# A fused decoder block on one core: weight sums of the head in shared buffers, attention values prepared later, scan outputs in the update's PSUM bank

## The chip, the core and the metric

The kernel runs on one core of a Trainium2 chip. The metric is device time in microseconds (us) of one execution. Each engine works through an instruction queue of its own in order: TensorE (PE in the profile) multiplies, VectorE (DVE) and ScalarE (ACT) work on elements and can read PSUM, the banks that TensorE writes, GpSimd (POOL) works on SBUF, and SyncE (SP) issues DMAs. Engines wait for each other by semaphores.

## The reference

One layer of a hybrid block, batch 1, 1024 tokens, width 1024, all float32. Two branches read the same normalised input:

```python
h = rmsnorm(x, norm_mix);  parts = split(h @ w_in)
# branch 1: forgetting attention, 8 heads of 128, softmax over causal logits with a decay bias
p = softmax(where(causal, q @ k.T * scale + (c[:, None] - c[None, :]), -inf));  y1 = p @ v
# branch 2: gated delta rule, 8 heads, in chunks of 64
u = u_hat - w @ state
o = q_dec @ state + attn @ u
state = state * g_last + k_dec.T @ u
# then: gated merge of the two branches with w_branch, w_out, residual, gated ConvFFN, final rmsnorm
```

## The kernel before

Every large product is made of three TensorE passes over operands that are split into a high and a low part (`split`, L106 the high part on ACT by a cast, L107 the low part by a subtraction on DVE or POOL). TensorE's instructions stand in the order in which the code issues them (`manual_schedule` at its engine); the other engines' orders are chosen by the tile scheduler from its own costs, except where `keep_in_program_order` pins an instruction. Waits follow from the tiles that instructions share; a PSUM tile here is a bank of 128x512 floats.

The stages, in us of the profiled span:

- **head_in**, 0 to about 143. Eight tiles of x are normalised and transposed. Token weights come in four groups `g` (tiles `vwr`, split into `vwh` on ACT and `vwl` on DVE or POOL); for each group `rows(g, t)` multiplies eight token tiles, 24 matmuls each (L570 to L572), and stores the result. Three generators are taken between these rows: `scalars()` (decays; its last part transposes `rt` on TensorE, L700), `block_sums` (L362, sums of blocks for the next stage), and `prepare_merge`. The last loads all of `w_branch` (16 tiles of 512 KB into `raw`, four buffers, L998), makes four sums for each pair of tiles on DVE (`weight_sums`, L982 to L985) and stores them to DRAM (`ms`, L1004), for a stage 1000 us later. Loads and stores of it are pinned in SP's order.
- **project**, about 143 to 830: the input projections by a Strassen scheme (products L156), weights streamed through `wr` (L125, three buffers of pool `stream`), split on ACT (`oh`) and POOL (`ol`), sums of weight blocks `ws` on DVE (L202).
- **mix**, about 830 to 1101: attention and scan woven together. `fox` yields 26 steps a head (`probs`: logits L1102 to L1104 into a small PSUM tile `ms`, a maximum by DVE L1109, exponentials on ACT L1115, scaling on ACT L1118 or, for late tiles `p`, on POOL L1121; `attend`: transposes L1142, splits into `ph` and `pl`, products L1133 into `ya`). `fox_values` prepares the values of a head after their load: `vf` a copy, `vh` a cast on ACT, `vl` a subtraction on POOL.
- Beside it run two `stream`s of the scan, four heads each, 8 chunks `n` a head. A chunk takes three steps. Step 1: `us[0:P]` = kT·st on TensorE (L1256), then DVE makes `sr` (L1258). Step 2: `us[P:2P]` = xt·r (L1261), ACT copies it to `su` (L1263), and TensorE puts qd·st into another bank, `op` (L1266). Step 3: `us[2P:3P]` = kt·u (L1269), DVE makes the next state `ss` from it (L1272, or a copy L1275 for the first chunk), TensorE adds aq·u to `op` (L1277), DVE copies `op` to `so` (L1278) and ACT squares it (`sjk`, L1280). From step 26 of the loop on, `mix` takes one step of one stream after each attention step, the streams by turns (L1341).
- PSUM in mix: `us` two banks, `op` two, `ya` one, `ms` three.
- Then merge, mix_out and the ConvFFN, to the end. The change does not touch their code.

Of the kernel before, what the change touches and what calls it, by code (L numbers as in the profile page):

```python
# [17 lines left out]
P = 128  # L18
# [69 lines left out]
class Block:  # L88
# [309 lines left out]
    def run(self):  # L398
        tc = self.tc

        def pool(stack, name, **kw):
            return stack.enter_context(tc.tile_pool(name=name, bufs=1, reuse_waits="tile", **kw))

        with ExitStack() as ctx:
            self.cp = ctx.enter_context(tc.tile_pool(name="const", bufs=1))
            self.dr = ctx.enter_context(tc.tile_pool(name="scratch", bufs=1, space=DRAM))
            self.constants()
            ctx.enter_context(tc.manual_schedule(engines={mybir.EngineType.PE}))
            psum, left, right = ExitStack(), ExitStack(), ExitStack()

            def banks(small, mm=0, conv=0):
                psum.close()
                if mm:
                    self.mm = pool(psum, "ps_mm", space=PSUM)
                else:
                    self.acc = pool(psum, "ps_acc", space=PSUM)
                self.ms = pool(psum, "ps_ms", space=PSUM)
                self.nms, self.nmm, self.ms_tag, self.ncv = small, mm, "ms", conv


            banks(8)
            blk = self.blocks(pool(right, "hn", side="right"), ("11", "21", "22"))
            blk = self.head_in(blk, right)
            banks(2, 4, 2)
            self.st = pool(right, "stream", side="right")
            self.wt = pool(right, "weights", side="right")
            self.nw = 4
            self.sx = pool(right, "sums", side="right")
            self.cx = pool(right, "outputs", side="right")
            self.nc_ = 3  # L430
            self.project(blk, lambda: pool(left, "fox_in"))
            right.close()

            banks(3)
            self.st = pool(ctx, "stream2", side="right")
            so, sc = ExitStack(), ExitStack()
            self.so = pool(so, "so", side="right")
            zs, bs = ExitStack(), ExitStack()
            self.z = []

            def merge_pools():
                left.close()
                self.wt = pool(ctx, "weights2")
                for half, stack in ((1, left), (0, zs)):
                    zp = pool(stack, f"z{half}")
                    self.z.insert(0, [zp.tile([P, 512], F32, name=f"z{half}{e}") for e in range(KD)])
                self.merge_first(pool(bs, "br0"))

            self.mix([pool(left, f"fox{i}") for i in range(4)], pool(sc, "scan", side="right"), merge_pools)
            sc.close()  # L450

            psum.close()
            self.mm = self.ms = pool(psum, "ps_merge", space=PSUM)
            self.nms, self.ms_tag = 4, "b"
            self.br.append(pool(bs, "br1"))

            def merge_last():
                so.close()
                self.br.append(pool(bs, "br2"))
            self.merge(merge_last)  # L460
            bs.close()
            banks(2, 6)
            first = ExitStack()
            blk = self.blocks(pool(right, "hn2", side="right"), ("22",))
            blk.update(self.blocks(pool(first, "hn2a", side="right"), ("11", "21")))
            jobs, lead, ready = self.mix_out(blk, zs, lambda: pool(left, "hn2t"))

            self.sx = self.cx = pool(left, "sums2")
            self.nc_ = 3
            rest = []  # L470

            def down_inputs():
                first.close()
                return pool(right, "down_in", side="right")

            def down_main():
                left.close()
                return pool(left, "down")
            down = self.ffn_down(down_inputs, down_main, blk["22"])
            self.ffn_up(pool(left, "up"), jobs, blk, lead, ready, rest, down)  # L480
            for r in rest:
                finish(r)
            psum.close()
            self.mm = pool(psum, "ps_mm3", space=PSUM)
            finish(down)
            left.close()
            right.close()
            psum.close()
# [52 lines left out]
    def head_in(self, blk, right):  # L541
# [3 lines left out]
        with tc.tile_pool(name="hin", bufs=1) as pool, ExitStack() as px:  # L545
# [8 lines left out]
            def wgroup(g, eng):  # L554
                wh = pool.tile([P, KD * VGW], F32R, tag="vwh", bufs=2, name="vwh")
                wl = pool.tile([P, KD * VGW], F32R, tag="vwl", bufs=2, name="vwl")
                for q in range(4):
                    sl = slice(q * 2 * VGW, (q + 1) * 2 * VGW)
                    wr = pool.tile([P, 2 * VGW], F32, tag="vwr", bufs=3, name="vwr")
                    nc.sync.dma_start(wr, a["w_tok"][g][:, sl])  # L560
                    self.split(wh[:, sl], wl[:, sl], wr, eng)
                return wh, wl
# [57 lines left out]
            sums = self.prepare_merge(pool)  # L620
            for g in range(1, NVG):
                w = wgroup(g, nc.gpsimd)
                take(scalars, 1)
                for t in range(NT):
                    rows(g, t, *w)
                    take(sums, 1)
                    if t % 4 == 2 and g < 3:
                        sl = slice((2 * (g - 1) + t // 4) * P, (2 * (g - 1) + t // 4 + 1) * P)
                        self.block_sums(blk, whole("12", sl), whole("22", sl), sl, pool)
# [4 lines left out]
    def scalars(self):  # L634
# [16 lines left out]
        with tc.tile_pool(name="scal", bufs=1) as pool:  # L651
# [24 lines left out]
            nc.tensor.matmul(ps[:, 0:P], self.tri, gf, start=True, stop=True)  # L676
            ps2 = self.small()
            nc.tensor.matmul(ps2[:, 0:P], self.ones, gf, start=True, stop=True)
            cum, tot = tw("cum"), tw("tot")
            v.tensor_copy(cum.rearrange("p h t -> p (h t)"), ps[:, 0:P])  # L680
            v.tensor_copy(tot.rearrange("p h t -> p (h t)"), ps2[:, 0:P])
            carry = tl("carry")
            nc.gpsimd.memset(carry, 0.0)
            for t in range(1, NT):
                v.tensor_tensor(carry[:, :, t:t + 1], carry[:, :, t - 1:t], tot[:, H:, t - 1:t], ALU.add)
            rt = tw("rt")
            v.tensor_copy(rt[:, 0:H], cum[:, 0:H])
            v.scalar_tensor_tensor(rt[:, H:], cum[:, H:], -1.0, carry, op0=ALU.mult, op1=ALU.subtract)
            v.tensor_copy(self.gc, cum[:, 0:H])
# [297 lines left out]
    def prepare_merge(self, pool):  # L987
# [5 lines left out]
        for br in range(2):  # L993
            for k in range(4):
                raws = []
                for half in range(2):
                    t = pool.tile([P, 1024], F32, tag="raw", bufs=4, name="raw")
                    self.tc.keep_in_program_order(nc.sync.dma_start(t, a["w_branch"][KD * br + 4 * half + k]))  # L998
                    raws.append(t)
                yield  # L1000
                r0, r1 = raws
                self.weight_sums(r0[:, left], r1[:, left], r0[:, right], r1[:, right])
                for d, t in zip(self.ms_d[br][k], raws):
                    self.tc.keep_in_program_order(nc.sync.dma_start(d, t))  # L1004
                yield
# [49 lines left out]
    def fox_values(self):  # L1055
        raw = self.vl.bitcast(F32)
        self.nc.gpsimd.tensor_copy(self.vf, raw[:, 3::4, :])
        for sl in (slice(0, 4), slice(4, 8)):
            self.split(self.vh[:, sl], self.vl[:, sl], raw[:, sl], self.nc.gpsimd)

    def fox_bias(self, h):
        nc = self.nc
# [101 lines left out]
    def fox(self, pools, scan_pool):  # L1164
# [5 lines left out]
        for h in range(H):  # L1170
            pts = [] if h else self.pts
            for t in range(len(pts), NT):
                yield from self.probs(h, t, pts)
                if t == (3 if h else 4):
                    self.fox_values()
            for half in range(2):
                for i, _ in enumerate(self.attend(h, half, pts)):
# [15 lines left out]
    def mix(self, fp, pool, before_last):  # L1193
        tc, nc, a = self.tc, self.nc, self.a
        self.yf_d, self.yg_d = ([self.dr.tile([P, S], F32, name=f"{n}{h}") for h in range(H)] for n in ("yfd", "ygd"))
        if True:
# [50 lines left out]
            def scan(h):  # L1247
# [2 lines left out]
                sumo = self.so.tile([P, NB], F32, tag="sumo", bufs=3, name="sumo")  # L1250
                st = None
                for n in range(NB):
                    us = self.acc.tile([P, 512], F32, tag="us", bufs=2, name="us")
                    r = vb[:, n, :]
                    if n:
                        nc.tensor.matmul(us[:, 0:P], kT[:, n, :], st, start=True, stop=True)  # L1256
# [4 lines left out]
                    nc.tensor.matmul(us[:, P:2 * P], xt[:, n, :], r, start=True, stop=True)  # L1261
                    u = pool.tile([P, P], F32, tag="su", bufs=4, name="su")
                    nc.scalar.copy(u, us[:, P:2 * P])  # L1263
                    op = self.acc.tile([P, 512], F32, tag="op", bufs=2, name="op")
                    if n:
                        nc.tensor.matmul(op[:, 0:P], qd[:, n, :], st, start=True, stop=False)  # L1266
                    yield
                    if n < NB - 1:
                        nc.tensor.matmul(us[:, 2 * P:3 * P], kt[:, n, :], u, start=True, stop=True)  # L1269
                        s2 = pool.tile([P, P], F32, tag="ss", bufs=6, name="ss")  # L1270
# [3 lines left out]
                        else:  # L1274
                            nc.vector.tensor_copy(s2, us[:, 2 * P:3 * P])  # L1275
                        st = s2
                    nc.tensor.matmul(op[:, 0:P], aq[:, n, :], u, start=(n == 0), stop=True)  # L1277
                    nc.vector.tensor_copy(o[:, n, :], op[:, 0:P])  # L1278
                    jk = pool.tile([P, P], F32, tag="sjk", bufs=1, name="sjk")
                    nc.scalar.activation(jk, op[:, 0:P], AF.Square, accum_out=sumo[:, n:n + 1])  # L1280
                    yield
                outs[h] = o, sumo

# [52 lines left out]
            while take(fox, 1):  # L1336
# [1 line left out]
                    preps[i > 0] = prep(int(i > 0))  # L1338
                    take(preps[i > 0], 1)
                if i >= 26:  # L1340
                    take(streams[i % 2], 1)  # L1341
                elif i >= 8 and i % 2:
                    take(streams[0], 1)
                i += 1
# [585 lines left out]
```

## Time and profile before

| what | us |
|---|---|
| median of three runs | 2029.84 (2026.92, 2033.71, 2029.84) |
| profiled execution | 2033.09 |
| its span | 2031.3 |
| TensorE busy in it | 1924.7 |
| DVE, ACT, POOL busy | 1468.3, 1076.7, 976.6 |
| span 826 to 1101 (mix): TensorE busy | 247.4 of 275 |
| span 105 to 150 (end of head_in): TensorE busy | 31.9 of 45 |

The page of the profile gives one execution. "Busy" of TensorE includes matmuls that overlap, and a granted clock below 1.00 makes matmuls longer without making TensorE idle. A timeline row gives start, duration, engine, line, operation, tiles, and in brackets how long the engine had been idle and who released it. Views of waits list, for each line that an engine waited at, the instruction that it waited for, with the total, the number of times and the longest wait.

### The profile page before, as it was taken

The page shows a single profiled execution, that of the slowest core. Times are in us where ns is not written, and L with a number is a line of the kernel's source. Part 1 is how long each engine was busy: PE and PEld are TensorE (multiplying, and loading weights), DVE is VectorE, ACT ScalarE, POOL GpSimd, SP SyncE. Part 2 cuts the span into 40 slices and gives each one's busy share as a digit, 9 for nine tenths or more (in the row PEclk, how much of TensorE's full clock was granted, in tenths as well). Part 3 has the DMA queues.
Part 4 walks back from the last instruction along what each step waited for, and adds up shares of the span by engine and source line. Part 5 has one row for each costly group of instructions (what it writes and reads, how often), then busy time and mean ns, then how long its engine had stood idle before and what let it go on. Part 6 is the DMA issues. An engine that isn't in the chain of part 4 may idle for free. (4 is left out here: it accounts for less than half of the span.)

```text
span 2031.3 us, 29170 instructions
## 1 busy us (share of the span) xinstructions
PE 1924.7 (95%) x9628; PEld 1605.3 (79%) x9628; DVE 1468.3 (72%) x2514; ACT 1076.7 (53%) x2354; POOL 976.6 (48%) x818
## 2 busy tenths in 40 slices
PE   7869999999999999898999899999999999999998
PEld 7867888888788788787888787777788888877886
DVE  8937677766999865576777798577866777777535
ACT  5325777763334454565666544466655555553234
POOL 5715665655555555356675143135566666530012
PEclk9979999999999999899999999999999999999999
DMA  4672444544333394765654853665343343368654
GB/s 163 202 274 84 153 146 128 159 148 150 119 106 116 104 316 163 239 218 184 209 205 133 297 172 109 200 211 166 137 142 134 110 151 120 114 231 328 219 191 161
DMA packets 179048, 350.95 MB, mean 173 GB/s; under 512 B 50448, under 2 KB 63056, under 8 KB 178896
## 3 DMA queue, kind: packets, MB, share of 16 engines
q1 hardware_dynamic: 178752, 348.56, 51.0%
q8 instruction: 76, 1.25, 0.3%
q10 hardware_dynamic: 144, 0.52, 0.1%
q14 instruction: 76, 0.62, 0.1%
HBM read 232.79 MB, written 116.23 MB: 172 GB/s over the span
## 5 line engine op out<-in xcount | busy, mean ns | idle before, releaser
L107 POOL TENSOR_TENSOR ol<-ws,oh 128x512 fp32r<-128x512 f32 x212 | 285.7, 1351 | 239.6 <-ACT oh L106 231.9
L107 POOL TENSOR_TENSOR ol<-wr,oh 128x512 fp32r<-128x512 f32 x165 | 230.0, 1397 | 280.6 <-ACT oh L106 199.0
L106 ACT CAST oh<-ws 128x512 fp32r<-128x512 f32 x212 | 130.9, 618 | 176.7 <-PE mm L156 165.0
L202 DVE TENSOR_TENSOR ws<-wr 128x512 f32<-128x512 f32 x106 | 106.7, 1007 | 152.1 <-DMA wr<-in_w_up_dram 73.3
L106 ACT CAST oh<-wr 128x512 fp32r<-128x512 f32 x204 | 123.5, 616 | 127.5 <-PE mm L156 79.1
L377 DVE SCALAR_TENSOR_TENSOR cv<-c,fw,cv 128x512 f32<-128x512 f32 (+2 forms) x176 | 127.4, 748 | 16.0 <-ACT cv L372 14.6
L377 DVE SCALAR_TENSOR_TENSOR cv<-c,cw,cv 128x511 f32<-128x511 f32 (+2 forms) x144 | 106.0, 749 | 6.2 <-ACT cv L372 4.3
L156 PE MATMUL mm<-b11h,oh 128*128 128x512 f32 x216 | 85.6, 396 | 12.9 <-ACT oh L106 12.9
L961 DVE TENSOR_TENSOR invt<-invz 128x399 f32<-128x399 f32 (+50 forms) x114 | 94.8, 846 | 0.4
L258 ACT COPY x<-mm 128x512 f32<-128x512 f32 x158 | 92.0, 582 | 5.4 <-PE mm L156 4.5
L156 PE MATMUL mm<-b22h,oh 128*128 128x512 f32 x216 | 85.9, 398 | 8.2 <-ACT x L258 8.2
L156 PE MATMUL mm<-bt1h,oh 128*128 128x512 f32 x216 | 85.2, 395 | 5.8 <-ACT x L258 5.7
L107 DVE TENSOR_TENSOR ol<-wd,oh 128x512 fp32r<-128x512 f32 x66 | 46.4, 706 | 58.7 <-ACT oh L106 58.7
L156 PE MATMUL mm<-bt4h,oh 128*128 128x512 f32 x216 | 85.5, 396 | 2.7 <-DVE c L300 2.7
L156 PE MATMUL mm<-bt4l,oh 128*128 128x512 f32 x216 | 86.3, 399 | 0.0
L156 PE MATMUL mm<-b22l,oh 128*128 128x512 f32 x216 | 86.1, 398 | 0.0
L156 PE MATMUL mm<-b21l,oh 128*128 128x512 f32 x216 | 86.0, 398 | 0.0
L156 PE MATMUL mm<-b11l,oh 128*128 128x512 f32 x216 | 85.7, 397 | 0.0
L156 PE MATMUL mm<-b11h,ol 128*128 128x512 f32 x216 | 85.3, 395 | 0.1
L156 PE MATMUL mm<-bt2l,oh 128*128 128x512 f32 x216 | 85.1, 394 | 0.3 <-DVE bt2l L107 0.3
L156 PE MATMUL mm<-bt1l,oh 128*128 128x512 f32 x216 | 84.9, 393 | 0.0
L156 PE MATMUL mm<-bt4h,ol 128*128 128x512 f32 x216 | 84.8, 392 | 0.0
(402 smaller groups left out, 6391.6 us busy)
## 6 DMA issues: line engine op xcount, KB each, us to landing
wr<-in_w_up_dram SPq DMA_DIRECT2D x43, 512.0 KB, 3.7
wr<-in_w_gdn_dram SPq DMA_DIRECT2D x24, 512.0 KB, 3.9
wr<-in_w_out_dram SPq DMA_DIRECT2D x24, 512.0 KB, 4.3
s<-hy SPq DMA_DIRECT2D x44, 256.0 KB, 3.1
s<-z SPq DMA_DIRECT2D x44, 256.0 KB, 3.6
wd<-in_w_down_dram SPq DMA_DIRECT2D x44, 256.0 KB, 5.9
b22h<-s SPq DMA_DIRECT2D x44, 256.0 KB, 2.8
b22l<-s SPq DMA_DIRECT2D x44, 256.0 KB, 3.2
```

Of the source, the lines that this page charges most:

```text
L106: nc.scalar.copy(hi, src)
L107: (lo_eng or nc.vector).tensor_tensor(lo, src, hi.bitcast(F32), ALU.subtract)
L156: self.nc.tensor.matmul(ps, lhs[:, sl], rhs[:, k, :], start=(first and k == 0 and i == 0), stop=(k == 3 and i == 2), skip_group_check=True)
L202: v.tensor_tensor(t, x, y, op)
L258: nc.scalar.copy(t, x)
L377: nc.vector.scalar_tensor_tensor(t[:, lo:], c[:, 512 * j + lo - s:512 * (j + 1) - s], w[:, n - 1 - s:n - s], t[:, lo:], op0=ALU.mult, op1= ...
L961: nc.vector.tensor_tensor(tv, z[:, m:n, 0:n].to_broadcast([P, r, n]), z[:, m, c0:c1].unsqueeze(2).to_broadcast([P, r, n]), ALU.mult))
```

## The change

Four edits, with no change to what is computed.

1. **Head.** The pool `stream` is opened before `head_in`. In `prepare_merge` every other pair of tiles (odd `k`) uses its `wr` buffers, three of them, and `raw` has two buffers in place of four; `vwr` has two in place of three. The sums are taken from row (1, 4) on, four rows later. The last part of `scalars` (transpose of `rt`) comes after row (3, 4) in place of ahead of group 3; three of its tiles reuse older ones.
2. **Attention values.** `fox_values` is called after the logits of tile 6 in place of tile 3 (4 for head 0), and the two casts to `vh` are pinned in ACT's order.
3. **Scan outputs.** `op` is no longer a bank of its own but the last quarter of `us`. `us` has three banks, `ms` four. The matmul qd·st moves from step 2 to step 3, behind kt·u and the reading of it by DVE.
4. **Streams.** From step 26 on, both streams take a step after every second attention step, in place of one stream after each.

```diff
@@ mix's banks
-            banks(3)
+            banks(4)
@@ wgroup
-                    wr = pool.tile([P, 2 * VGW], F32, tag="vwr", bufs=3, name="vwr")
+                    wr = pool.tile([P, 2 * VGW], F32, tag="vwr", bufs=2, name="vwr")
@@ head_in
-                take(scalars, 1)
+                if g < 3:
+                    take(scalars, 1)
                 for t in range(NT):
                     rows(g, t, *w)
-                    take(sums, 1)
+                    if g > 1 or t > 3:
+                        take(sums, 1)
+                    if (g, t) == (3, 4):
+                        finish(scalars)
@@ prepare_merge
-                    t = pool.tile([P, 1024], F32, tag="raw", bufs=4, name="raw")
+                    if k % 2 == 0:
+                        t = pool.tile([P, 1024], F32, tag="raw", bufs=2, name="raw")
+                    else:
+                        t = self.st.tile([P, 1024], F32, tag="wr", bufs=3, name="raw")
@@ fox_values
-            self.split(self.vh[:, sl], self.vl[:, sl], raw[:, sl], self.nc.gpsimd)
+            self.tc.keep_in_program_order(self.nc.scalar.copy(self.vh[:, sl], raw[:, sl]))
+            self.nc.gpsimd.tensor_tensor(self.vl[:, sl], raw[:, sl], self.vh[:, sl].bitcast(F32), ALU.subtract)
@@ fox
-                if t == (3 if h else 4):
+                if t == 6:
                     self.fox_values()
@@ scan
-                    us = self.acc.tile([P, 512], F32, tag="us", bufs=2, name="us")
+                    us = self.acc.tile([P, 512], F32, tag="us", bufs=3, name="us")
...
-                    op = self.acc.tile([P, 512], F32, tag="op", bufs=2, name="op")
-                    if n:
-                        nc.tensor.matmul(op[:, 0:P], qd[:, n, :], st, start=True, stop=False)
                     yield
+                    old = st
                     if n < NB - 1:
                         nc.tensor.matmul(us[:, 2 * P:3 * P], kt[:, n, :], u, start=True, stop=True)
...
-                    nc.tensor.matmul(op[:, 0:P], aq[:, n, :], u, start=(n == 0), stop=True)
-                    nc.vector.tensor_copy(o[:, n, :], op[:, 0:P])
+                    op = us[:, 3 * P:]
+                    if n:
+                        nc.tensor.matmul(op, qd[:, n, :], old, start=True, stop=False)
+                    nc.tensor.matmul(op, aq[:, n, :], u, start=(n == 0), stop=True)
+                    nc.vector.tensor_copy(o[:, n, :], op)
@@ mix
                 if i >= 26:
-                    take(streams[i % 2], 1)
+                    if i % 2:
+                        for s in streams:
+                            take(s, 1)
```

In the changed file the scan's lines are L1264 (kT·st), L1266 (`sr`), L1269 (xt·r), L1271 (`su`), L1275 (kt·u), L1278 and L1281 (`ss`), L1285 (qd·st), L1286 (aq·u), L1287 (`so`), L1289 (`sjk`); the logits are L1110 to L1112, the casts to `vh` L1066.

TensorE's queue in the middle of mix, where each stream ends a chunk. Before, xt·r and qd·st of one stream (L1261, L1266), then logits and four transposes (L1302), then step 3 of the first stream, logits, step 3 of the second:

```order
L1261 MATMUL us<-sr,sxt 128x128 [waits DVE_49]
L1266 MATMUL op<-ss,sqd 128x128 [waits Activation_49]
L1302 MATMUL ms<-ident,so 128x128 [waits DVE_49,PE_49,Pool_49]
L1302 MATMUL ms<-ident,so 128x128 x3
L1102 MATMUL ms<-kh,qh 128x320 [waits DVE_49,PE_49]
L1103 MATMUL ms<-kl,qh 128x320
L1104 MATMUL ms<-kh,ql 128x320
L1269 MATMUL us<-su,skt 128x128 [waits Activation_49]
L1277 MATMUL op<-su,saq 128x128
L1102 MATMUL ms<-kh,qh 128x384 [waits DVE_49]
L1103 MATMUL ms<-kl,qh 128x384
L1104 MATMUL ms<-kh,ql 128x384
```

And now:

```order
L1110 MATMUL ms<-kh,qh 128x384 [waits DVE_49]
L1111 MATMUL ms<-kl,qh 128x384
L1112 MATMUL ms<-kh,ql 128x384
L1275 MATMUL us<-su,skt 128x128 [waits Activation_49]
L1285 MATMUL us<-ss,sqd 128x128 [waits DVE_49]
L1286 MATMUL us<-su,saq 128x128
L1275 MATMUL us<-su,skt 128x128 [waits Activation_49]
L1285 MATMUL us<-ss,sqd 128x128 [waits DVE_49]
L1286 MATMUL us<-su,saq 128x128
L1110 MATMUL ms<-kh,qh 128x384 [waits PE_49]
L1111 MATMUL ms<-kl,qh 128x384
L1112 MATMUL ms<-kh,ql 128x384
```

Both streams' step 3 stand together, qd·st has moved behind kt·u, and it now waits for DVE, where the aq·u that stood in its place waited for nothing. What it waits for is DVE's reading of the bank's third quarter (L1278), which the matmul just ahead of it has filled. This wait stands at 48 matmuls L1285 and, for the first chunk of each head, at 8 matmuls L1286 (behind L1281).

ACT's queue at the values of the fourth attention head. `vh` and `vl` are the values, `p` the probabilities of a tile, `su` the scan's copy. Before:

```order
L1118 ACTIVATE p_9621<-p_9621,mm 128x128 [waits DVE_49]
L106 CAST vh<-vl 128x512 [waits DMAHW5_49]
L106 CAST vh<-vl 128x512
L1115 ACTIVATE p_9650,mm<-p_9650,mm 128x256 [waits DVE_49,Pool_49]
L1263 COPY su<-us 128x128 [waits PE_49]
L1115 ACTIVATE p_9667,mm<-p_9667,mm 128x384 [waits DVE_49,Pool_49]
```

And now:

```order
L1123 ACTIVATE p_9697,mm<-p_9697,mm 128x768 [waits DVE_49]
L1271 COPY su<-us 128x128 [waits PE_49] x2
L106 CAST ph<-ms 128x512 [waits PE_49]
L1123 ACTIVATE p_9732,mm<-p_9732,mm 128x896 [waits DVE_49]
L1066 CAST vh<-vl 128x512 [waits DMAHW4_49]
L1066 CAST vh<-vl 128x512
L1123 ACTIVATE p_9788,mm<-p_9788,mm 128x1024 [waits DVE_49]
```

The two casts, and with them the wait for the values' load, moved from behind the first tile's probabilities to behind the seventh's.

SP's queue at the end of head_in: stores of the sums (`ms`), stores of the rows (`vd`), and the first three weight loads of the next stage (`wr`). Before:

```order
L1004 DMA ms_689<-raw 128x1024 [waits DMAHW2_49,DVE_49]
L580 DMA vd<-vev 128x262 [waits DMAHW3_49,Activation_49]
L1004 DMA ms_690<-raw 128x1024 [waits DMAHW4_49,DVE_49]
L1004 DMA ms_691<-raw 128x1024 [waits DMAHW6_49,DMAHW5_49,DVE_49]
L580 DMA vd<-vev 128x262 [waits Activation_49]
L580 DMA vd<-vev 128x262 [waits DMAHW7_49,Activation_49]
L580 DMA vd<-vev 128x262 [waits DMAHW0_49,Activation_49]
L125 DMA wr<-in_w_gdn_dram 128x1024 [waits DMAHW1_49,Pool_49]
L125 DMA wr<-in_w_gdn_dram 128x1024 [waits DMAHW2_49,PE_49]
L125 DMA wr<-in_w_gdn_dram 128x1024 [waits DMAHW3_49]
```

And now:

```order
L125 DMA wr<-in_w_gdn_dram 128x1024 [waits DMAHW5_49]
L580 DMA vd<-vev 128x262 [waits DMAHW4_49,Activation_49]
L1010 DMA ms_825<-raw 128x1024 [waits DVE_49]
L580 DMA vd<-vev 128x262 [waits DMAHW6_49,Activation_49]
L1010 DMA ms_826<-raw 128x1024 [waits DMAHW7_49,DVE_49]
L1010 DMA ms_827<-raw 128x1024 [waits DMAHW0_49,DVE_49]
L1010 DMA ms_828<-raw 128x1024 [waits DMAHW1_49,DVE_49]
L713 DMA gr<-rows 128x512 [waits DMAHW2_49,PE_49]
L713 DMA gr<-rows 128x512 [waits DMAHW3_49]
L125 DMA wr<-in_w_gdn_dram 128x1024 [waits DMAHW4_49,DMAHW0_49]
L125 DMA wr<-in_w_gdn_dram 128x1024 [waits DMAHW5_49,DMAHW1_49]
```

The first of the three loads moved ahead of the last four stores of the sums; the second and third stand behind them, and now wait for stores out of the buffers that they fill.

More of the change, by code (lines that the diff above doesn't have):

```diff
@@ L422, in run @@
             blk = self.blocks(pool(right, "hn", side="right"), ("11", "21", "22"))
+            self.st = pool(right, "stream", side="right")
             blk = self.head_in(blk, right)
             banks(2, 4, 2)
-            self.st = pool(right, "stream", side="right")
             self.wt = pool(right, "weights", side="right")
@@ L678, in scalars @@
             nc.tensor.matmul(ps2[:, 0:P], self.ones, gf, start=True, stop=True)
-            cum, tot = tw("cum"), tw("tot")
+            cum, tot, rt = z, az, e
             v.tensor_copy(cum.rearrange("p h t -> p (h t)"), ps[:, 0:P])
@@ L685, in scalars @@
                 v.tensor_tensor(carry[:, :, t:t + 1], carry[:, :, t - 1:t], tot[:, H:, t - 1:t], ALU.add)
-            rt = tw("rt")
             v.tensor_copy(rt[:, 0:H], cum[:, 0:H])
@@ L1276, in scan @@
                         st = s2
-                    nc.tensor.matmul(op[:, 0:P], aq[:, n, :], u, start=(n == 0), stop=True)
-                    nc.vector.tensor_copy(o[:, n, :], op[:, 0:P])
+                    op = us[:, 3 * P:]
[3 more added lines that the diff above has]
+                    nc.vector.tensor_copy(o[:, n, :], op)
                     jk = pool.tile([P, P], F32, tag="sjk", bufs=1, name="sjk")
-                    nc.scalar.activation(jk, op[:, 0:P], AF.Square, accum_out=sumo[:, n:n + 1])
+                    nc.scalar.activation(jk, op, AF.Square, accum_out=sumo[:, n:n + 1])
                     yield
```

## The prediction

> **What bounds the kernel now.** I read the page first: the busy line.
>
> ```profile
> PE 1924.7 (95%) x9628; PEld 1605.3 (79%) x9628; DVE 1468.3 (72%) x2514; ACT 1076.7 (53%) x2354; POOL 976.6 (48%) x818
> ```
>
> TensorE is busy for 1924.7 of 2031.3 us. The change removes no matmul, so it can act only on the 106.6 us in which TensorE is idle, on the few us at a lower clock, or by adding idle time. Idle time in TensorE's queue is end-to-end time, since nothing overtakes in it. The second view is the table of windows over the stages that are edited (columns: length; busy time of PE, PEld, DVE, ACT, POOL with counts; granted clock; DMA share; GB/s).
>
> ```profile
> 50.00:105.00 55.00, 47.04 (x385) 46.85 (x384) 54.58 (x64) 19.89 (x42) 43.05 (x26) 0.94 0.56 189
> 105.00:135.00 30.00, 25.20 (x192) 25.00 (x190) 11.18 (x17) 3.79 (x10) 0.00 (x0) 0.90 0.96 347
> 135.00:150.00 15.00, 6.72 (x22) 4.97 (x23) 4.04 (x4) 4.79 (x9) 5.55 (x4) 0.61 0.63 210
> 826.00:1101.00 275.00, 247.40 (x1751) 223.13 (x1750) 191.26 (x711) 180.13 (x507) 157.60 (x173) 0.96 0.60 197
> ```
>
> Mix has 27.6 us of idle TensorE in 275, the head some 21 between 50 and 150. The third view is the list of TensorE's waits, first for the end of the head, then for mix (total, times, longest).
>
> ```profile
> PE mm L156 <- ACT oh L106: 12.9, 1, 12.9
> PE ms L700 <- DVE rt L688: 8.0, 1, 8.0
> ```
>
> ```profile
> PE us L1269 <- ACT su L1263: 8.3, 5, 3.9
> PE ms L1142 <- POOL p L1121: 4.8, 4, 2.5
> PE ms L1142 <- DVE pl L107: 4.3, 7, 2.0
> PE ms L1102 <- DVE mx L1109: 1.8, 4, 0.8
> ...
> PE us L1256 <- DVE ss L1272: 0.3, 1, 0.3
> ```
>
> So mix's idle time is scattered over short waits, the longest group being kt·u, which waits for ACT's copy `su`. DVE's update `ss` is hardly waited for (0.3). The view of its line says how long DVE itself sat idle for it.
>
> ```profile
> L1272 DVE SCALAR_TENSOR_TENSOR ss<-ss,egl,us x48: 328/342/350, 856.6 to 1099.4; 128x128 f32<-128x128 f32 x48
> its engine sat idle before it (us, times) until:
>   PE us L1269: 10.8, 8
> ```
>
> **Scan outputs in the bank of the update.** This is the term that decides. Before, the order was kt·u, then at once aq·u into another bank; DVE turned kt·u into `ss` meanwhile, and `ss` was needed a step later. Now qd·st writes the bank that DVE is reading, and the order rows of the change show it waiting for DVE; it stands directly behind kt·u. So TensorE has nothing to do from the end of kt·u to the end of `ss`, 56 times (48 at L1285, 8 at L1286 for first chunks). The trace of before holds this round trip, only not as a wait. Three cases from the timeline, with kt·u (L1269), aq·u (L1277) and `ss`:
>
> ```profile
> 916.49 0.38 PE L1269 MATMUL us<-su,skt 128*128 128x128 f32 x2
> 916.71 0.39 PE L1277 MATMUL op<-su,saq 128*128 128x128 f32 x2
> 916.91 0.35 DVE L1272 SCALAR_TENSOR_TENSOR ss<-ss,egl,us 128x128 f32<-128x128 f32 x1 [0.23 <-PE us L1269]
> ...
> 945.37 0.58 PE L1269 MATMUL us<-su,skt 128*128 128x128 f32 x2
> 945.74 0.64 PE L1277 MATMUL op<-su,saq 128*128 128x128 f32 x2
> 946.13 0.33 DVE L1272 SCALAR_TENSOR_TENSOR ss<-ss,egl,us 128x128 f32<-128x128 f32 x1
> ...
> 1026.50 2.19 DVE L1049 SCALAR_TENSOR_TENSOR ql<-ql,qh 128x1024 fp32r<-128x1024 f32 x1 [1.47 <-ACT qh L1048]
> 1027.00 0.39 PE L1277 MATMUL op<-su,saq 128*128 128x128 f32 x2
> 1028.82 0.33 DVE L1272 SCALAR_TENSOR_TENSOR ss<-ss,egl,us 128x128 f32<-128x128 f32 x1
> ```
>
> The stall is the end of `ss` less the time at which the next matmul started. In the first case DVE was idle and waiting: 916.91 + 0.35 - 916.71 = 0.55 us. That is the floor. In the second DVE came 0.17 us later than that: 946.13 + 0.33 - 945.74 = 0.72. In the third an operation of 2.19 us stood ahead: 2.15. DVE was idle and waiting in only 8 of the 48 cases. Lower bound: 56 x 0.55 = 31 us. Upper: the same difference, row by row over all 56 pairs; the first and the last:
>
> ```profile
> 847.82 0.63 PE L1277 MATMUL op<-su,saq 128*128 128x128 f32 x2
> 848.06 0.29 DVE L1275 COPY ss<-us 128x128 f32<-128x128 f32 x1
> ...
> 1099.15 0.39 PE L1277 MATMUL op<-su,saq 128*128 128x128 f32 x2
> 1099.35 0.35 DVE L1272 SCALAR_TENSOR_TENSOR ss<-ss,egl,us 128x128 f32<-128x128 f32 x1 [1.36 <-PE us L1269]
> ```
>
> They give 0.53 and 0.55, and the 56 sum to 47.6, a mean of 0.85. I take 0.72, the second case and near the middle of 0.55 and 0.85, since DVE catches up on its queue while TensorE stands: **+40 us**.
>
> Could it cost nothing? Only if the wait were not there or were met beforehand. The trace shows that engines are kept apart by bank and not by need:
>
> ```profile
> ACT sjk L1280 <- DVE so L1278: 11.6, 10, 1.8
> ```
>
> ACT squares what DVE copies, both only read `op`, and still ACT waited 10 times for the copy. The Trainium skill ("PSUM — Partial Sum Buffer", section "PSUM bank collisions raise a hardware error") states the rule: two engines may not touch the same bank and partitions at once, not even in separate columns, so guard by bank. By that rule the sum contains the +40; by the address alone, under which the fourth quarter is free while the third is read, the term would be 0 and the total some 20 us below the time before. No run here shows a collision.
>
> What else belongs to this part: the third `us` bank and the fourth `ms` bank add slack. The wait of the transposes L1142 for `pl` (4.3) is a wait for a small bank to come free, so a fourth one takes most of it. The waits for `mx` (1.8) and for POOL's `p` (4.8) are waits for engines that run behind; TensorE, coming 40 us later over the stage, meets part of them done. Of these 10.9 us I take away **-9**, with 0 and -19 (mix's whole idle time less the 8.3 below) as ends.
>
> **Attention values later.** The list of ACT's waits in mix, then the timeline at the longest wait of kt·u:
>
> ```profile
> ACT vh L106 <- DMA vl<-vd: 12.4, 6, 4.4
> ```
>
> ```profile
> 942.45 1.14 ACT L106 CAST vh<-vl 128x512 fp32r<-128x512 f32 x2 [4.41 <-DMA vl<-vd]
> 944.29 0.49 PE L1269 MATMUL us<-su,skt 128*128 128x128 f32 x2 [3.93 <-ACT su L1263]
> ```
>
> ACT stands at the cast for the values' load, `su` is queued behind, TensorE behind that. With the cast three tiles of logits later (six of the 205 attention steps that fill the 275 us, so some 8 us), the load is there and the wait goes: nearly all of the 8.3 us, **-8**. What is late next is `vl`: its two subtractions on POOL (16 of them, 1280 ns each) now stand among the scalings of `p` for the last tiles, and the first product with `vl` follows soon after.
>
> ```profile
> L107 POOL TENSOR_TENSOR vl<-vl,vh 128x512 fp32r<-128x512 f32 x16 | 20.1, 1280 | 7.3 <-issue 4.9 <-ACT vh L106 2.4
> ```
>
> Two subtractions put the last scaling off by up to 2.6 us in each of seven heads, 18 us at worst; but POOL is idle for 117 of 275 us, and by then TensorE has 8 transposes and a few products to do that need neither. **+2**, with 0 and +6 as the ends I hold likely. Where the clock drops after the 3.93 us wait (below) another 1 us comes back: **-1**.
>
> **Streams together.** The number of steps is the same, and each stream still moves once in two attention steps. The pairing takes away the attention matmuls that stood between the two round trips, so the second one gets no cover from the first; this is in the 56. It is counted at nothing otherwise.
>
> **Head.** The waits of 8.0 and 12.9 are the targets. The rows:
>
> ```profile
> 101.64 1.83 POOL L107 TENSOR_TENSOR vwl<-vwr,vwh 128x524 fp32r<-128x524 f32 x1
> 104.39 0.45 PE L700 MATMUL ms<-ident,rt 128*128 128x128 f32 x1 [7.96 <-DVE rt L688]
> 132.65 1.05 SPq L1004 DMA_DIRECT2D ms<-raw  x2
> 138.10 1.35 SPq L125 DMA_DIRECT2D wr<-in_w_gdn_dram  x3
> 143.15 0.80 PE L156 MATMUL mm<-b11h,oh 128*128 128x512 f32 x1 [12.95 <-ACT oh L106]
> ```
>
> Without the transpose ahead of group 3, TensorE can start its rows when the last `vwl` is there. That was at 103.47, 0.9 us before it started anyway; with DVE relieved of the sums for four rows, this chain comes some 4 us earlier, and TensorE may finish its rows up to 8 us sooner. But the stage ends with the weights of project. Between 105 and 135 the DMA share is 0.96: 16.8 MB of `w_branch` in and out must pass (16 tiles of 512 KB each way), no less than before, and they start four rows later. One of the three first weight loads now passes ahead of the last stores, the other two stand behind them and must wait for stores out of their own buffers. Before, the first product came 5 us behind the issue of its load (143.15 - 138.10); with an issue near 130, ahead of the last stores, it would come at 135. The third, which needs a sum of two later weights, comes hardly earlier. I take **-3.5**, with +2 (loads later by the delay of the sums) and -9 as ends. Two buffers for `vwr` in place of three may cost 0.5 at the start.
>
> **Sum.** 40 - 9 - 8 + 2 - 1 - 3.5 + 0.5 = +21. On the profiled execution's 2033.09 that is 2054; on the median of 2029.84, 3.25 lower, it is **2051 us**, which is my forecast. A change under 0.3%, about 6 us (2023.7 to 2035.9), cannot be told from none here.
>
> **Rivals.** *The round trip is hidden, and the kernel gets faster.* Mechanism: at L1285 TensorE waits only for what is left of `ss`. If loading of weights and the pipeline's drain covered all but 0.2 us, the term is 11, and the sum 11 - 9 - 8 + 2 - 1 - 3.5 + 0.5 = -8, or with the head's better end -13.5: 2016 to 2022. It decides at (9 + 8 - 2 + 1 + 3.5 - 0.5) / 56 = 0.34 us for each round trip. Against it: the `ss` alone takes 0.34, and DVE's start after kt·u comes on top. 0.14.
>
> *The floor holds and the waits of before vanish.* 31 for the stalls, but mix's other waits go wholly (-19): 31 - 19 - 8 + 2 - 1 - 3.5 + 0.5 = 0 to +2, no change that can be told: 2030 to 2032. 0.09.
>
> *The clock falls as well.* After the wait of 3.93 the clock went down, after another of 1.35 it did not:
>
> ```profile
> 944.00:947.00 3.00, 2.71 (x14) 2.71 (x15) 2.54 (x14) 3.00 (x13) 3.00 (x4) 0.74 1.03 411
> 1010.00:1013.00 3.00, 3.00 (x21) 2.93 (x22) 3.00 (x15) 3.00 (x10) 1.11 (x1) 1.00 0.96 339
> ```
>
> A stall of 0.7 is too short for that alone, but two round trips stand side by side, with 0.6 us of matmuls between, and the upper ends are near 2 us. If a fall of some 3 us at half clock came ten times, at 1.5 us each, it would add 15: 2066. 0.12. The Trainium skill ("TensorE: Matmul & The Clock Gate") gives about 3.4 us as the idle window after which the clock is halved; by it the paired stalls cost no clock, which is why this is a rival and not the forecast.
>
> *The head's edit does nothing or harm* (+2 for -3.5): 2056, inside the forecast's range.
>
> **How the numbers follow.** Forecast 0.60 (own range 2038 to 2062: 0.55 to 0.85 us a round trip is -9 to +8, the rest the head and the absorbed waits), clock 0.12, no change 0.09, faster 0.14; 0.05 for a cost that I do not see, mostly on the slow side. Slower 0.77, same 0.09, faster 0.14. The range of 8 in 10 reaches from 2024, which leaves out most of the faster rival, to 2068.
>
> **What would show it.** In the changed profile the list of TensorE's waits in mix should have the lines L1285 <- DVE `ss` and L1286 <- DVE at its top, together 30 to 45 us, and mix should be 20 to 30 us longer with more idle TensorE; the wait of L1275 for `su` should be under 2 us, and `vh` <- DMA small. The first product of project should start near 135, with new waits for `ws` or `ol` before 150. I am wrong if those two lines sum to under 19 us (faster then), if mix's clock is under 0.93 (rival three), or if `vl` or the last `p` on POOL heads the list.

## The result and the profile after

The changed kernel is slower: 2065.44 us (2064.65 to 2067.66) against 2031.1 of the kernel before (four runs now), a ratio of 1.0173 with a 95% interval of 1.0153 to 1.0193. The forecast was slower, 2051, with a range of 2024 to 2068. One execution in this document, of the kernel with the head's edit alone, took 2935.40 at a granted clock of 0.61; its ratio leaves it out.

The profiled execution took 2066.07 with a span of 2064.4, 33.1 longer than before. Landmarks on TensorE place it: attention's last product came at 1099.8 before and at 1132.0 now, the first scan product of mix at 844.0 before and 840.6 now. So mix took 291.4 us in place of 255.8, **35.6 more**, what lies ahead of it 3.4 less, and what follows 0.9 more.

TensorE's waits in mix of the changed kernel (total, times, longest), to be held against the list of before:

```profile
PE us L1285 <- DVE ss L1278: 31.7, 46, 1.4
PE us L1275 <- ACT su L1271: 4.0, 2, 2.1
PE us L1286 <- DVE ss L1281: 3.4, 7, 1.0
...
PE ya L1141 <- POOL vl L1067: 1.8, 2, 1.2
...
PE us L1285 <- DVE mm L1122: 1.1, 2, 0.5
PE ya L1141 <- DVE pl L107: 0.8, 3, 0.5
...
PE us L1285 <- ACT su L1271: 0.7, 1, 0.7
PE ms L1110 <- DVE mx L1117: 0.7, 1, 0.7
PE us L1286 <- DVE mm L1122: 0.7, 1, 0.7
```

The two lines of the prediction head the list: at qd·st (L1285) and the first chunks' aq·u (L1286) TensorE waited 31.7 + 3.4 + 1.1 + 0.7 + 0.7 = 37.6 us. Of these, 36.9 stand at the 56 matmuls behind kt·u; the 0.7 put down to ACT stand at the last chunk of a head, where there is no kt·u. The waits of the transposes for `p` (4.8) are gone and those for `pl` fell from 4.3 to 0.8; kt·u's wait for `su` is halved, 8.3 to 4.0. Two such waits are left. At both, ACT has just made a late cast to `vh` (at 842.33 and 1077.85, 1.12 us for its two parts, with no wait for the load), ahead of the copy to `su`:

```profile
843.67 0.79 PE L1275 MATMUL us<-su,skt 128*128 128x128 f32 x2 [2.09 <-ACT su L1271]
...
1079.93 0.49 PE L1275 MATMUL us<-su,skt 128*128 128x128 f32 x2 [1.92 <-ACT su L1271]
```

But 36.9 less what vanished does not make 35.6. The windows over the same stretch of the program, before and after (length; busy time of PE, PEld, DVE, ACT, POOL; clock), show the rest:

```profile
843.50:1100.00 256.50, 233.35 (x1665) 212.44 (x1666) 179.49 (x666) 169.05 (x486) 151.50 (x167) 0.95 0.59 191
```

```profile
840.00:1132.30 292.30, 242.98 (x1666) 214.25 (x1666) 185.88 (x666) 172.86 (x489) 155.60 (x170) 0.96 0.52 169
```

TensorE's idle time rose from 23.2 to 49.3, 26.1 more, and its *busy* time rose by 9.6 with the same matmuls and no lower clock. Rows of one step tell why; kt·u, `ss`, qd·st:

```profile
904.60 0.39 PE L1275 MATMUL us<-su,skt 128*128 128x128 f32 x2
905.35 0.34 DVE L1278 SCALAR_TENSOR_TENSOR ss<-ss,egl,us 128x128 f32<-128x128 f32 x1
905.74 0.49 PE L1285 MATMUL us<-ss,sqd 128*128 128x128 f32 x2 [0.76 <-DVE ss L1278]
```

The pair at 904.60 ends at 904.99, but in an unbroken row the next pair would have started 0.22 after it, at 904.82 (as at 916.49 and 916.71 before). It started at 905.74: 0.92 late, of which the profile calls 0.76 idle. The other 0.16 is the pair's tail, which a following matmul would have overlapped. Over all 56 steps the lateness, row by row, sums to 46.7 us, 0.83 a step. So 46.7 came in, and to make 35.6 some 11.1 must have gone. The lists agree: outside the 56, TensorE idled for 23.2 before and for 49.3 - 36.9 = 12.4 now, 10.8 less.

### The profile page after: what moved, and what is told of

It is laid out like the page before. It is cut to its first block, busy times and chain, and to the rows that moved or that the text cites. A ratio compares the mean times of both kernels' runs of the same rounds, so it can differ in the third digit from the quotient of the medians.

```text
span 2064.4 us, 29115 instructions
## 1 busy us (share of the span) xinstructions
PE 1935.3 (94%) x9628; PEld 1607.5 (78%) x9628; DVE 1460.2 (71%) x2514; ACT 1078.8 (52%) x2354; POOL 973.5 (47%) x818
## 5 line engine op out<-in xcount | busy, mean ns | idle before, releaser
L202 DVE TENSOR_TENSOR ws<-wr 128x512 f32<-128x512 f32 x106 | 100.8, 951 | 149.6 <-DMA wr<-in_w_up_dram 78.0
L156 PE MATMUL mm<-bt2h,oh 128*128 128x512 f32 x216 | 84.5, 391 | 1.7 <-ACT oh L106 1.7
L156 PE MATMUL mm<-bt2h,ol 128*128 128x512 f32 x216 | 84.2, 390 | 1.0 <-POOL ol L107 1.0
```

What stands on the lines that cost most here:

```text
L156: self.nc.tensor.matmul(ps, lhs[:, sl], rhs[:, k, :], start=(first and k == 0 and i == 0), stop=(k == 3 and i == 2), skip_group_check=True)
L202: v.tensor_tensor(t, x, y, op)
```

## Experiments

"Ratio" is to the kernel before on the same chip, with its 95% interval.

### The wait taken out, in two ways, and put in alone

The first kernel gives `op` its own bank again and leaves the other three edits:

```diff
-            banks(4)
+            banks(3)
-                    us = self.acc.tile([P, 512], F32, tag="us", bufs=3, name="us")
+                    us = self.acc.tile([P, 512], F32, tag="us", bufs=2, name="us")
...
+                    op = self.acc.tile([P, 512], F32, tag="op", bufs=2, name="op")
+                    if n:
+                        nc.tensor.matmul(op[:, 0:P], qd[:, n, :], st, start=True, stop=False)
                     yield
...
```

> The changed kernel with the scan outputs back in a bank of their own (two banks us, two op, three ms, and the product of the query with the state back in step 2); the head, the later values and the streams together stay. Theory (the wait of 56 matmuls for DVE's reading of the same bank is the whole loss, 47 us with the overlap that each of them breaks): the lines L1285/L1286 <- DVE vanish, the time falls by 47 less up to 12 for older waits that the stalls had absorbed: 2018 to 2030. Rival one (streams stepping together cost the time, as no attention stands between their products): stays over 2045. Rival two (later values put POOL's work in the way): stays over 2045, with waits for vl or p at the top.

Measured: 2040.98, ratio 1.0030 (1.0013 to 1.0047). The wait's lines vanished and 1.4% came back, but the kernel stayed slower than before, well above the range. Both rivals' "over 2045" failed too, but the sign that rival two named, `vl` at the top, is there:

```profile
PE ya L1141 <- POOL vl L1067: 11.3, 6, 4.2
PE us L1277 <- ACT su L1271: 4.1, 4, 1.9
PE ms L1150 <- DVE pl L107: 3.4, 4, 1.9
```

The products with `vl` now wait for POOL's subtractions, 11.3 us where the changed kernel had 1.8.

The second kernel keeps the shared bank and moves only the order of issue within step 3:

```diff
+                    op = us[:, 3 * P:]
                     if n < NB - 1:
                         nc.tensor.matmul(us[:, 2 * P:3 * P], kt[:, n, :], u, start=True, stop=True)
+                    if n:
+                        nc.tensor.matmul(op, qd[:, n, :], old, start=True, stop=False)
+                    nc.tensor.matmul(op, aq[:, n, :], u, start=(n == 0), stop=True)
+                    if n < NB - 1:
                         s2 = pool.tile([P, P], F32, tag="ss", bufs=6, name="ss")
...
-                    op = us[:, 3 * P:]
-                    if n:
-                        nc.tensor.matmul(op, qd[:, n, :], old, start=True, stop=False)
-                    nc.tensor.matmul(op, aq[:, n, :], u, start=(n == 0), stop=True)
```

> The changed kernel with one thing moved: in step 3 TensorE's three products (update, query with state, attention with u) are issued ahead of DVE's reading, so that all banks are as in the changed kernel but no matmul waits for DVE within the step. Theory: the 56 waits vanish, DVE's ss comes 0.4 us later and nobody waits for it: 2014 to 2026, below the kernel before. Rival one: over 2045, since the streams still step together. A third way: ss is late then and the next step's product kT with the state waits for it, which would give back up to 20 us: 2030 to 2045.

Measured: 2034.08, ratio 1.0014 (0.9999 to 1.0028), above the theory's range. The time lies in that of the third way, but not by its mechanism: the DVE waits within the step are gone, and `ss`, read later, is waited for once, for 0.2 us. Again the sum of the "gains" that should remain is missing, and again `vl` heads the list:

```profile
PE ya L1141 <- POOL vl L1067: 7.4, 3, 4.3
PE us L1276 <- ACT su L1271: 6.2, 4, 1.9
PE ms L1150 <- POOL p L1129: 4.4, 3, 2.6
PE us L1264 <- ACT sjk L1290: 3.9, 2, 2.9
```

The last line is a cost of the shared bank itself: `op` now holds a bank of `us` until ACT has squared it, and kT·st of a later chunk waited for that bank 3.9 us where the kernel before shows no such wait.

The third kernel is the one before with the sharing alone (the diff's parts in `scan` and `banks`).

> The kernel before with the scan-output edit alone (op in the last quarter of us, three banks us, four ms, the query's product behind the update's); head, values and turns as before. Theory: 2031 + 47 less some 8 for waits that are absorbed, 2062 to 2078, with 56 waits for DVE of 35 to 40 us in the list. Rival one (it is the stepping together): 2031 to 2045. Rival two (values): 2031 to 2045.

Measured: 2083.09, ratio 1.0244 (1.0219 to 1.0269), above the theory's range.

```profile
PE us L1277 <- DVE ss L1270: 30.0, 45, 1.4
PE ya L1133 <- DVE pl L107: 4.9, 5, 1.7
PE us L1267 <- ACT su L1263: 4.5, 4, 2.3
PE us L1278 <- DVE ss L1273: 4.4, 7, 1.2
```

Mix took 303.9 us (843.4 to 1147.3), 48.1 more than before. That this is near the prediction's upper end for the stalls alone (47.6) does not mean that nothing was absorbed: its waits at these two lines are 37.2, its other idle time 17.8 where it was 23.2 before, and TensorE's busy time rose by 16.2, more than in the changed kernel, at a clock of 0.94. So one edit alone costs more than all four together.

### The other three edits, each alone on the kernel before, and the streams by turns

By turns means the changed kernel with its last edit undone:

```diff
-                    if i % 2:
-                        for s in streams:
-                            take(s, 1)
+                    take(streams[i % 2], 1)
```

> The changed kernel with the streams by turns again, all else kept. Theory: the round trip is the same for each step wherever it stands, 2058 to 2070, with 35 to 40 us of waits at L1285 and L1286. Rival one (the stepping together is the loss): 2018 to 2040.

Measured: 2072.55, ratio 1.0189 (1.0164 to 1.0213), 2.5 us above the theory's range. Pairing the streams is not the loss. The converse, the paired step alone on the kernel before:

> The kernel before with the streams stepping together alone. Theory: it counts for nothing by itself, 0.998 to 1.002. Rival (two scan steps side by side leave too little work between the links of a chain, so that sr, su and ss are waited for): 1.003 or more, with waits at kT with the state or at xt.

Measured: 2029.89, ratio 0.9995 (0.9981 to 1.0008): nothing.

The head's edit alone (the first of the four):

> The kernel before with the head's edit alone. Theory now (from the traces: the first product of project 6 us earlier, the third no earlier, as its weights are issued 3 us later): 0.999 to 1.002. Rival (the prediction's term, -3.5): 0.996 to 0.999.

Measured: 2029.6, ratio 0.9996 (0.9983 to 1.0009). It can't be told from nothing; the prediction's -3.5 (0.9983) lies at the edge of the interval. The traces of before and of the changed kernel show how the gain at the first product is lost. Before, SP's loads and TensorE:

```profile
138.10 1.35 SPq L125 DMA_DIRECT2D wr<-in_w_gdn_dram  x3
...
143.15 0.80 PE L156 MATMUL mm<-b11h,oh 128*128 128x512 f32 x1 [12.95 <-ACT oh L106]
...
157.09 0.50 PE L156 MATMUL mm<-bt1h,oh 128*128 128x512 f32 x1 [0.83 <-ACT x L258]
```

After:

```profile
131.47 0.33 SPq L125 DMA_DIRECT2D wr<-in_w_gdn_dram  x1
...
141.06 10.32 SPq L125 DMA_DIRECT2D wr<-in_w_gdn_dram  x3
...
136.99 0.80 PE L156 MATMUL mm<-b11h,oh 128*128 128x512 f32 x1 [13.73 <-ACT oh L106]
140.97 0.79 PE L156 MATMUL mm<-b11h,ol 128*128 128x512 f32 x1 [2.76 <-POOL ol L107]
150.49 0.50 PE L156 MATMUL mm<-bt2h,oh 128*128 128x512 f32 x1 [1.69 <-ACT oh L106]
152.18 0.50 PE L156 MATMUL mm<-bt2h,ol 128*128 128x512 f32 x1 [0.96 <-POOL ol L107]
157.32 0.39 PE L156 MATMUL mm<-bt1h,oh 128*128 128x512 f32 x1
```

The first product came 6.2 us earlier, since its load passed the stores. The next loads were issued at 141.06, 3 us later than before; three waits of 2.8, 1.7 and 1.0 follow, and by 157 the same product runs 0.2 later than before. Over all traces it starts at 156.7 to 158.5 in the five kernels with the old head and at 155.5 to 160.7 in the eight with the new one. The 2.6 us by which project ended early in the changed kernel's execution came elsewhere, from a wait of before that it did not have, and from the lower clock about that wait (0.79 and 0.87 in the ten us from 550, where the changed kernel had 1.00):

```profile
552.95 0.80 PE L156 MATMUL mm<-bt4h,oh 128*128 128x512 f32 x1 [2.26 <-DVE c L300]
```

This is not shown to be the head's doing: five of the eight traces with the new head have this wait too, and where it is missing, as here, an earlier one at the same line is longer (1.88 at 494.84, where it was 0.44 before).

The later attention values alone:

```diff
-            self.split(self.vh[:, sl], self.vl[:, sl], raw[:, sl], self.nc.gpsimd)
+            self.tc.keep_in_program_order(self.nc.scalar.copy(self.vh[:, sl], raw[:, sl]))
+            self.nc.gpsimd.tensor_tensor(self.vl[:, sl], raw[:, sl], self.vh[:, sl].bitcast(F32), ALU.subtract)
...
-                if t == (3 if h else 4):
+                if t == 6:
```

> The kernel before with the later attention values alone. Theory now (from the two runs without the wait, where products waited 7 to 11 us for vl): the waits for su behind the cast go (about -7), but POOL's subtractions to vl stand among the scalings of the last tiles and TensorE waits for vl instead (+7 to +11): 0.998 to 1.004 of before, vl at the top of the list. Rival (the sum of the prediction, -8 for su and +2 for vl): 0.995 to 0.998.

Measured: 2041.22, ratio 1.0057 (1.0039 to 1.0075). Worse than either theory: this edit, which the prediction credited with 7, costs 11.6 us by itself (0.0057 of 2031). The profiled execution took 2050.40, the longest of the six (the others 2039.84 to 2042.51), so its lists show more than the usual loss.

```profile
PE ya L1134 <- POOL vl L1060: 10.2, 6, 3.4
PE us L1270 <- ACT su L1264: 6.7, 5, 5.1
...
PE ms L1143 <- POOL p L1122: 2.2, 1, 2.2
```

```profile
844.00:1100.00 256.00, 227.76 (x1590) 208.51 (x1588) 173.63 (x652) 161.52 (x461) 141.25 (x156) 0.92 0.58 188
```

```profile
851.24 0.80 PE L1270 MATMUL us<-su,skt 128*128 128x128 f32 x2 [5.10 <-ACT su L1264]
...
959.92 0.80 PE L1134 MATMUL ya<-ph,vl 128*128 128x512 f32 x1 [3.38 <-POOL vl L1060]
```

`vl` is waited for 10.2 us. Of the wait for `su`, 5.1 is now a single one at the start of mix, where ACT stood 1.73 and 1.21 at the casts of the next head's `kh` and `qh` for their loads; the other four are short, so behind the casts of the values it did go. The clock in mix is 0.92 where it was 0.95: the product behind the wait of 3.38 takes 0.80, where its kind took 0.41 on average before. Over the whole execution all six runs lie at 0.977 to 0.983, those of the kernel before at 0.982 to 0.989.

### The sharing without the wait, alone, and the sum of what is left

The kernel before with the shared bank and TensorE's three products first:

> The kernel before with the scan outputs in the update's bank, but TensorE's three products ahead of DVE's reading; head, values and turns as before. Theory: the sharing costs nothing once no matmul waits for a reader of its bank, and the fourth small bank takes the 4 us of waits for pl: 0.996 to 1.000, where the sharing with the wait gave 1.024. Rival (the shared bank itself costs, by the later ss or by the three-bank ring): over 1.004.

Measured: 2027.42, ratio 0.9981 (0.9968 to 0.9995). The same banks are no loss here once no product within the step stands behind DVE's reading: this kernel and the one at 1.0244 differ in that order alone. The head, the paired streams and this sharing, with the values as before (the second kernel above with the edit to the values undone):

> The head's edit, the streams together and TensorE's three products first, with the attention values as before (tile 3): all edits but the late values, without the wait. Theory (the wait and the late values are the only losses; head and streams together are worth nothing, the fourth small bank 0.2%): 0.995 to 0.999 of before, no waits for vl. Rival (some other interplay of the edits costs time, since the two kernels without the wait stood at 1.001 and 1.003): 1.001 or more.

Measured: 2023.98 (before: 2030.84), ratio 0.9963 (0.9947 to 0.9979). It beats both kernels. Against 1.0014 with the late values it is 0.5% better; so without the wait, the late values are a loss.

Between the two, the values behind tile 5:

> The same with the attention values behind the logits of tile 5 in place of 6, the casts pinned: ACT's cast comes some 5 us later than before, POOL's subtractions to vl ahead of the scalings of tiles 6 and 7. Theory (late enough for the load, early enough for POOL): waits for su at the update fall to 3 or less and those for vl stay under 3, 0.992 to 0.997. Rival (POOL has no slack for the subtractions anywhere behind tile 3): vl is still waited for, over 5 us, 1.000 or more.

Measured: 2030.77, ratio 0.9999 (0.9985 to 1.0013). The theory failed, and the rival came near, with `vl` at 4.7 and not over 5: POOL's subtractions moved ahead of two scalings, and TensorE waited most for the scaled `p`, 7.2 where it was 4.4 with tile 6.

```profile
PE ms L1150 <- POOL p L1129: 7.2, 5, 2.5
PE ya L1141 <- POOL vl L1067: 4.7, 4, 3.2
PE us L1276 <- ACT su L1271: 4.6, 5, 1.5
```

Last, the changed kernel, its 56 waits included, with early values:

> The changed kernel with the attention values early again, all else as changed, the 56 waits included. Theory (TensorE's stalls give POOL the time for vl, so that beside them the late cast costs nothing and its gain, the waits for su, shows): 2068 to 2078, above the changed kernel, though the late values alone made the kernel before 0.6% slower. Rival (the late values cost here too): 2050 to 2062.

Measured: 2072.55, ratio 1.0193 (1.0177 to 1.0210), in the theory's range, though the interval overlaps that of the changed kernel (1.0153 to 1.0193). The four together (head and paired streams in all):

| | values early | values late |
|---|---|---|
| three products first, no wait | 0.9963 | 1.0014 |
| 56 waits for DVE | 1.0193 | 1.0173 |

The wait costs 2.3% with early values and 1.6% with late ones. Beside the wait the late values cost nothing, without it half a per cent. The waits for `vl` go with it: 1.8 us in the changed kernel, 7.4 without the wait. POOL's work is the same in both; that TensorE's stalls are what gives it the time is the reading that fits, and was not tried by itself.

One thing stays open. The sharing alone stood at 1.0244; with the head's edit and the paired streams beside it, the values early in both, it stands at 1.0193, some 10 us less, though each of these two edits alone is worth nothing. No run separates what makes this difference.

## Why the prediction was right in its sign and short in its size

- *The wait at L1285 decides.* Right: 46 + 7 waits for `ss` and 3 put down to `mm` make 56, and most of the loss goes when the wait goes (1.0030 and 1.0014), by either way of taking it out. The rule that engines are kept apart by bank was borne out as a wait in this program; what happens without the wait was not tried.
- *+40 for it.* The mechanism held, the term was mis-sized: 46.7. The prediction measured the end of `ss` less the next start, row by row, and had 47.6 as its upper end; it then took 0.72 a step because DVE would catch up while TensorE stands. DVE caught up by half of that: up to the end of `ss` the 56 now sum to 43.7, a mean of 0.78 against 0.85 before. The other 3.0 are a term that the prediction left out: the released matmul starts 0.05 after the end of `ss`, each time. The lists of waits would have hidden the size, since they show 36.9; the rest lies in matmuls that count as busy.
- *-9 for waits that are met, -8 and -1 for `su`, +2 for `vl`.* The sum was -16, the trace shows about -11. `p` and `pl` went as said. The load of the values is indeed there: ACT's wait for it (12.4) is gone from its list, and so are the four waits for `su` behind that cast. But these were 6.9 us, not "nearly all of the 8.3"; the fifth, 1.4 at the start of mix, stood behind the cast of `kh`. And the late cast itself still stands ahead of `su` in ACT's queue, at the two waits that are left. So `su` kept 4.0, where under 2 was forecast. The step that failed is the price of the values, -7 in all: alone the late cast costs 11.6, with `vl` late by 10.2 where +2 was allowed, with +6 as the end held likely. In the changed kernel `vl` was near its forecast (1.8); that the stalls covered it was not tried by itself.
- *Head -3.5.* Not found: 0.9996 alone. The first product came 6 us sooner (137.0, forecast 135), and the third paid for it, as two loads stood behind the last stores; the end "+2" named this mechanism, and the measured ratio (-0.8, with an interval of -3.5 to +1.8) lies between the two.
- *Clock.* The rival fell: 0.96 in mix. The 3.4 us of idle time that the prediction names is no safe bound here, though: the clock fell after the single wait of 2.26 at 552.95 (0.79, then 0.87) and not after that of 1.88 at 494.84 (1.00).
- *Faster, by a hidden round trip of 0.2.* Fell: the smallest lateness was 0.50.
- The sum: 46.7 - 11.1 in mix, 3.4 less ahead of it and 0.9 more behind it make 33; the forecast had 24 in mix and 3 less ahead of it. Mix was to be 20 to 30 us longer and was 35.6. The sign and its cause were foreseen; that the time fell inside the wide range owes something to luck. It lies above the forecast's own range (to 2062) and next to the 2066 of the rival of the clock, whose mechanism did not happen.

## What to carry to other kernels

Before an output moves into a bank that another engine reads, look at what TensorE issues next into that bank: the order of issue, all of TensorE's products first and the readers behind them, made the difference between 1.0244 and 0.9981 with the same banks. Price a round trip by the delay of the next start, not by the idle time in the list of waits. And test an edit alone before crediting it: one that removes a wait may put another engine's work in its place, and a stall elsewhere may cover that until it is mended.

## What the runs showed of the hardware that was not expected

A break in a row of 128x128 matmuls costs more than the idle time that the profile shows for it: 46.7 us of lateness over 56 breaks stand as 36.9 of idle, the other 0.17 a break being the tail of the pair ahead, which counts as busy. In mix TensorE's busy time rose by 9.6 us with no more work and no lower clock (0.95 before, 0.96 now). The two kernels without the wait show no such rise: 234.0 and 234.5 busy in mix, against 233.4 before and 243.0 with it.
